# Wide weight units, earlier first loads and moved side work in a two-layer encoder step

## The chip, the cores and the metric

The kernel runs on one core of a Trainium2 chip. Five engines work in parallel, each with its own instruction queue that is taken strictly in order: TensorE (matrix products and transposes into PSUM), VectorE and ScalarE (element work), GpSimd (element work and some DMA issues), and SyncE (SP), which issues most DMAs. The metric is device time in microseconds, of the whole program. Three runs of the kernel before gave 2964.94, 2965.09 and 2965.37 us.

## The reference

Two groups of tokens, a prompt of 256 and a sample of 64, go through two layers with the same weights; here they are one block of 320 columns. All is in fp32.

```python
# layer 0: one projection, then A (8 query heads, 2 key heads, rotary, window 128, sinks)
#          and B (8 heads, own chunk + 8 before, relative bias), one output projection
h = x @ w_in_ab ; qa, ka = rope(...), rope(...)
out = concat(band_attention(A), band_attention(B)) @ w_out_ab
# layer 1: low-rank queries and keys with a rotary part, chunk-causal attention
# every layer:
x = layer_norm(ALPHA * x + mix, ln1_g, ln1_b)
x = layer_norm(ALPHA * x + square(relu(x @ w_up)) @ w_down, ln2_g, ln2_b)
gate = sigmoid(x @ w_ple_gate + b_ple_gate)
x = x + gate * (p @ w_ple)
```

The model width is 2048 (16 k-blocks of 128), the hidden width 8192. Outputs are the two results and the new caches.

## The kernel before, in words

**Layout.** Activations lie transposed: a tile has 128 features on the partitions and 320 tokens as columns. Each product is made of three matmuls: a value is split into a high part (a ScalarE copy to the rounded format fp32r) and a low part (a VectorE subtraction), and high x high, high x low and low x high are summed in PSUM. In names, `hl` is such an activation pair, `sf` and `t` are plain fp32 tiles, `mm` and `ax` are PSUM banks (five and three), `st` holds statistics.

**Weights.** `Weights` holds a list of units in the order of use. A unit has 128 rows times 1024 numbers: `wr` is what a DMA brought (four buffers), `ws` the split pair (four buffers). A unit is split in two slices of 512 numbers for each partition; `hi` is the ScalarE half and `lo` the VectorE half of one. `pump` emits such halves between the matmuls of the units before, `split_next` emits one, and `need` those that a matmul is about to use.

**Groups.** `group` computes 4 column blocks (128 features each) over all k-blocks, 12 matmuls for each k-block. `group8` does 8 column blocks at once, 24 matmuls for each k-block; it is used where the input appears tile by tile behind a norm: the first up projection and the first half of the gate, in both layers. Its units are planned by `plan_pair`: two units side by side, each of 2 k-blocks by 512 columns.

**Order.** The program is written out by a planner, `Sched`: it keeps an estimated clock for each engine (a VectorE operation of 320 columns counts 0.41 us), and side work is a generator that gives back when it wants to go on. `sch.tick()` after each few matmuls lets due generators emit their next instructions. Nothing of these times is in the program: only the order is, and an engine runs an instruction as soon as its inputs are there.

**Norms.** `ln_finish` sums the columns by matmuls with `ones` (`colsum`), copies the sums to `st`, takes the root, spreads mean and scale over the partitions by transposes (`tokbcast`), and emits products of the small matrix `w_ple` (`fill`) on TensorE between these steps.

**Rotation.** `rope` copies the bank to a tile (ScalarE), makes the swapped and multiplied halves by GpSimd (`u`), and multiplies and adds on VectorE. In layer 0 it runs for the two key heads (`akv_done`) and eight query heads (`aq_done`), in layer 1 for the rotary parts.

**Gate.** `gate_done` for tile `mt`: sigmoid (ScalarE), one product and two additions (VectorE), then a split for layer 1, or, in the last layer, transposes and output stores.

**Layer 1.** `residual` adds the two parts of each of the 16 inputs of layer 1 on GpSimd, for the output projection much later. It is added to the planner behind the group `cq`.

**Start.** `load_x` brings x in four pieces of 512 columns, three tiles each; `trans_x` transposes one k-block of it, `x_ready` keeps two k-blocks ahead of the first group, `akv`.

Of the kernel before, what the change touches and what calls it, by code (L numbers as in the profile page):

```python
# [33 lines left out]
KT = 16  # L34
# [142 lines left out]
class Weights:  # L177
# [23 lines left out]
    def plan_pair(self, key, w, c0):  # L201

        for r in range(0, D, 256):
            for h in range(2):
                a = w[r:r + 256, c0 + h * 512:c0 + (h + 1) * 512]
                self.unit(key, a.rearrange("(k p) c -> p k c", p=128), 2, 512)
# [9 lines left out]
    def dma(self):  # L216
# [6 lines left out]
        else:  # L223
            self.k.nc.sync.dma_start(out=t, in_=a)
# [3 lines left out]
    def hi(self):  # L228
        i, k0, k1 = self.slices[self.nhi]
        while self.ndma <= i:  # L230
            self.dma()
        if k0 == 0:
# [4 lines left out]
        self.k.S.activation(out=self.spl[i][:, 0, k0:k1], in_=self.raw[i][:, k0:k1], func=AF.Copy)  # L237
# [4 lines left out]
    def lo(self):  # L242
        i, k0, k1 = self.slices[self.nlo]
# [5 lines left out]
        self.k.V.tensor_tensor(out=s[:, 1, k0:k1], in0=r[:, k0:k1], in1=f32(s[:, 0, k0:k1]), op=ALU.subtract)  # L249
        self.nlo += 1  # L250
        sch.ready = keep
        if k1 == self.units[i][2]:
            del self.raw[i]
# [21 lines left out]
    def take(self, key):  # L275
        self.cur += 1
        assert self.units[self.cur][0] == key, (self.units[self.cur][0], key)
        self.spl.pop(self.cur - 1 - self.lag, None)
# [3 lines left out]
    def need(self, kk):  # L282

        while self.nlo < len(self.slices):
            i, k0, k1 = self.slices[self.nlo]
# [10 lines left out]
def trunk_kernel(ctx: ExitStack, tc: tile.TileContext, a, o):  # L296
# [116 lines left out]
    def plan_mlp(i):  # L413
        for c in range(8):
            if c == 0:
                ws.plan_pair(f"up{i}0", a["w_mlp_up"][i], 0)
# [10 lines left out]
        ws.plan_pair(f"gate{i}0", a["w_ple_gate"][i], 0)  # L427
# [82 lines left out]

    def load_x(ch):
        for j in range(3):
            t = slot_f((128, 512))
            n = 128 if j < 2 else 64
            if j == 2:
                G.memset(t[64:], 0.0)
            src = a["x_prompt"][0, j * 128:(j + 1) * 128] if j < 2 else a["x_sample"][0]
            nc.sync.dma_start(out=t[:n], in_=src[:, ch * 512:(ch + 1) * 512])
# [5 lines left out]
    ws.dma()  # L524
    ws.dma()
    ws.dma()
    load_x(1)
    ws.dma()

# [107 lines left out]
    def group8(key, rhs, done, need):  # L637

        ps = []
        ws.lag = 1  # L640
        for i in range(KT):
            need(i)
            kk = i % 2
            if kk == 0:
                ws.take(key)
                w0 = ws.spl[ws.cur]
                w1, _ = ws.take(key)
            ws.need(kk)
            ws.pump(2)
            x = rhs(i)  # L650
            w = lambda u, mm: (w0, w1)[mm // 4][:, u, kk, mm % 4 * 128:mm % 4 * 128 + 128]
# [1353 lines left out]
```

## Time and profile before

| | us |
|---|---|
| median of 3 runs | 2965.09 |
| the profiled execution | 2965.06 |
| its span | 2963.3 |
| TensorE busy in it | 2930.4 |
| VectorE / ScalarE / GpSimd busy | 1737.1 / 1299.4 / 221.6 |
| read from HBM, mean rate | 418.22 MB, 145 GB/s |

The span is the time from the first to the last recorded instruction. Busy times say which engine is the densest, not what each wait costs; for that the waits of TensorE are to be read, and the stretches in which its granted clock is 0.5 (1.2 GHz) instead of 1.0 (2.4 GHz). Before 14.45 us no clock is recorded, so the first stretch is read from the spacing of matmuls.

### The profile page before, as it was taken

To read this page: it belongs to the slowest core of one execution; us is meant where nothing else is said; L and a number is where in the kernel's file an instruction comes from. 1 tells how busy PE (TensorE), PEld (TensorE's weight loads), DVE (VectorE), ACT (ScalarE), POOL (GpSimd) and SP (SyncE) were. 2 spreads that over 40 slices of the span, in tenths; PEclk is the share of its full clock that TensorE was granted. 3 is DMA by queue.
4 is the path that set the end of the run, shared out by engine and by line. 5 is a ranking of instruction groups with operands and counts; after the bars stand their busy time and mean duration, and the time that the engine had idled before them with its cause. 6 is when DMAs were issued, how large, how long until landed. Compare 5 with 4: busy or idle time off the path is not lost.

```text
span 2963.3 us, 51140 instructions
## 1 busy us (share of the span) xinstructions
PE 2930.4 (99%) x20241; PEld 2922.5 (99%) x20241; DVE 1737.1 (59%) x3446; ACT 1299.4 (44%) x2745; POOL 221.6 (7%) x290
## 2 busy tenths in 40 slices
PE   9999999999999999999999999999999999999999
PEld 8999999999999999999999999999999999999998
DVE  5666677544444444557667676775444444444675
ACT  4455445344343343345455455453343343343453
POOL 2110020000000000011003110200000000000201
PEclk9999999999999999999999999999999999999999
DMA  7445444544444444444453323454444444444444
GB/s 237 135 152 166 150 142 137 164 149 146 155 150 148 153 150 151 150 137 145 144 149 112 102 79 105 130 158 154 149 147 151 155 146 145 161 149 144 143 146 118
DMA packets 284496, 430.17 MB, mean 145 GB/s; under 512 B 34518, under 2 KB 110024, under 8 KB 284256
## 3 DMA queue, kind: packets, MB, share of 16 engines
q1 hardware_dynamic: 280224, 416.75, 45.0%
q0 software_dynamic: 4032, 10.16, 1.0%
q8 instruction: 158, 2.59, 0.3%
q14 instruction: 82, 0.67, 0.1%
HBM read 418.22 MB, written 10.72 MB: 145 GB/s over the span
## 4 chain that ended last, share of the span: by engine, by line
PE 96%; DVE 2%; ACT 1%; DMA 1%; issue 0%; SPq 0%; ACTq 0%; POOL 0%; DVEq 0%; POOLq 0%
PE mm L386 27%; PE mm L388 27%; PE mm L387 27%; PE mm L664 1%; PE mm L663 1%; PE mm L665 1%; PE mm L620 1%; PE ax L402 1%; DVE t L172 1%; PE ax L664 1%; PE ax L663 1%; PE ax L665 1%; PE ax L388 1%; PE ax L387 1%; PE ax L386 0%
## 5 line engine op out<-in xcount | busy, mean ns | idle before, releaser
L386 PE MATMUL mm<-hl,ws 128*128 128x320 f32 x5608 | 1746.1, 311 | 1.9 <-DVE qz L172 1.3
L388 PE MATMUL mm<-hl,ws 128*128 128x320 f32 x5608 | 1733.4, 309 | 4.4 <-DVE ws L172 4.4
L387 PE MATMUL mm<-hl,ws 128*128 128x320 f32 x5608 | 1732.7, 309 | 0.0
L172 DVE TENSOR_TENSOR ws<-wr,ws 128x512 fp32r<-128x512 f32 (+1 forms) x1568 | 1045.1, 702 | 607.0 <-ACT ws L172 600.2
L172 ACT ACTIVATE ws<-wr 128x512 fp32r<-128x512 f32 (+1 forms) x1568 | 912.5, 620 | 1113.6 <-PE mm L388 860.8
L388 PEld LDWEIGHTS mm<-hl,ws 128*128 128x128 f32 x5608 | 1054.7, 188 | 5.2 <-DVE ws L172 5.2
L386 PEld LDWEIGHTS mm<-hl,ws 128*128 128x128 f32 x5608 | 1055.4, 188 | 4.1 <-DVE sf L172 1.8
L387 PEld LDWEIGHTS mm<-hl,ws 128*128 128x128 f32 x5608 | 1055.6, 188 | 0.0
L172 DVE TENSOR_TENSOR sf<-sf,mm 128x320 f32<-128x320 f32 x272 | 123.4, 487 | 204.6 <-PE mm L388 204.1
L172 POOL TENSOR_TENSOR t<-sf 128x320 f32<-128x320 f32 x8 | 7.5, 940 | 1871.6 <-DVE sf L172 1871.6
L172 DVE TENSOR_TENSOR t<-t 128x320 f32<-128x320 f32 x128 | 58.2, 489 | 123.3 <-ACT t L172 123.3
L665 PE MATMUL mm<-hl,ws 128*128 128x320 f32 x300 | 92.7, 309 | 0.0
L663 PE MATMUL mm<-hl,ws 128*128 128x320 f32 x300 | 92.7, 309 | 0.0
L664 PE MATMUL mm<-hl,ws 128*128 128x320 f32 x300 | 92.7, 309 | 0.0
L172 POOL TENSOR_TENSOR t<-t,sf 32x320 f32<-32x320 f32 (+2 forms) x72 | 77.4, 1074 | 197.5 <-ACT t L172 156.3
L172 ACT ACTIVATE t<-mm 128x320 f32<-128x320 f32 (+1 forms) x141 | 61.3, 435 | 50.2 <-PE mm L388 43.9
L172 DVE TENSOR_TENSOR sf<-sf,t 128x320 f32<-128x320 f32 x131 | 77.4, 612 | 2.9 <-ACT t L172 2.9
L172 ACT ACTIVATE hl<-ax 128x256 fp32r<-128x256 f32 (+3 forms) x110 | 33.0, 328 | 104.0 <-PE ax L402 42.7
L172 DVE TENSOR_TENSOR hl<-ax,hl 128x256 fp32r<-128x256 f32 (+3 forms) x110 | 36.4, 353 | 66.7 <-ACT hl L172 66.0
L172 DVE TENSOR_TENSOR hl<-t,hl 128x320 fp32r<-128x320 f32 (+1 forms) x152 | 68.8, 481 | 0.1
L172 ACT ACTIVATE hl<-t,PC 128x320 fp32r<-128x320 f32 x64 | 36.0, 563 | 72.4 <-DVE t L172 72.4
L172 ACT ACTIVATE hl<-t 128x320 fp32r<-128x320 f32 (+1 forms) x152 | 64.8, 461 | 6.1 <-DVE t L172 5.8
(162 smaller groups left out, 2042.7 us busy)
## 6 DMA issues: line engine op xcount, KB each, us to landing
wr<-in_w_mlp_up_dram SPq DMA_DIRECT2D x256, 512.0 KB, 3.7
wr<-in_w_mlp_down_dram SPq DMA_DIRECT2D x256, 512.0 KB, 4.1
wr<-in_w_ple_gate_dram SPq DMA_DIRECT2D x64, 512.0 KB, 3.7
wr<-in_w_in_ab_dram SPq DMA_DIRECT2D x114, 256.0 KB, 3.1
wr<-in_w_out_ab_dram SPq DMA_DIRECT2D x32, 512.0 KB, 3.9
wr<-in_w_out_c_dram SPq DMA_DIRECT2D x32, 512.0 KB, 3.8
wr<-in_w_kv_b_c_dram SPq DMA_DIRECT2D x16, 512.0 KB, 3.7
wr<-in_w_in_ab_dram SPq DMA_DIRECT2D x15, 512.0 KB, 5.1
```

The costliest lines, as they stand in the source:

```text
L172: return f(*args, **kw)
L386: P.matmul(out, wh, xh, start=start, stop=False)
L387: P.matmul(out, wh, xl, start=False, stop=False)
L388: P.matmul(out, wl, xh, start=False, stop=stop)
L402: P.transpose(out, in_, ident if n == 128 else ident[:n, :n])
L620: P.matmul(ps[mm][:, :T], w[:, u, kk, mm * 128:(mm + 1) * 128], x[:, v], start=z, stop=False)
L663: P.matmul(o_, w(0, mm), x[:, 0], start=False, stop=False)
L664: P.matmul(o_, w(1, mm), x[:, 0], start=False, stop=False)
L665: P.matmul(o_, w(0, mm), x[:, 1], start=False, stop=i == KT - 1)
```

## The change

- `plan_wide` takes the place of `plan_pair`: a unit is one k-block by 1024 columns, and its slices are the two column halves. `group8` takes one unit for each k-block. In `ln_finish` one more `split_next` stands ahead of the copy of the sums.
- `gate_done` gives back for 2000 ns times the tile's number ahead of its VectorE work, for the first eight tiles; the wait ahead of the last layer's transposes is gone.
- `rope_p` takes the place of `rope` in layer 0: the two halves are swapped by two ScalarE copies out of PSUM, and all products are VectorE's.
- `residual` is added behind `ckv`, ahead of `ckr` and `cq`, with a delay of 1000 in place of 3000.
- The first pieces of x have 256 columns; two weight units are issued from ScalarE's queue; 20 transposes of the identity stand first on TensorE; only one k-block of x is transposed ahead of the first split; the memsets of x tiles go to VectorE.

```diff
+    def plan_wide(self, key, w, c0):
+        for r in range(0, D, 128):
+            self.unit(key, w[r:r + 128, c0:c0 + 1024].rearrange("(k p) c -> p k c", p=128), 1, 1024)
...
-        step = max(1, SLICE // ncols)
+        step, wide = max(1, SLICE // ncols), min(SLICE, ncols)
         for k0 in range(0, nk, step):
-            self.slices.append((i, k0, min(nk, k0 + step)))
+            for c0 in range(0, ncols, wide):
+                self.slices.append((i, k0, min(nk, k0 + step), c0, c0 + wide))
...
+    XC = (0, 256, 512, 1024, 1536, 2048)
     load_x(0)
-    ws.dma()
-    ws.dma()
-    ws.dma()
+    ws.dma(nc.scalar)
+    ws.dma(nc.scalar)
     load_x(1)
     ws.dma()
+    load_x(2)
+    ws.dma()
+    warm = aux()
+    for _ in range(20):
+        P.transpose(warm[:, 0:128], ident, ident)
+    free()
...
     def group8(key, rhs, done, need):
         for i in range(KT):
             need(i)
-            kk = i % 2
-            if kk == 0:
-                ws.take(key)
-                w0 = ws.spl[ws.cur]
-                w1, _ = ws.take(key)
-            ws.need(kk)
+            w, _ = ws.take(key)
+            ws.need(0)
             ws.pump(2)
...
+    def rope_p(src, tab, dst, u):
+        copy(u[0:64], src[64:128, :T])
+        copy(u[64:128], src[0:64, :T])
+        V.tensor_tensor(out=dst, in0=src[:, :T], in1=tab[:, 0], op=ALU.mult)
+        yield
+        V.tensor_tensor(out=u, in0=u, in1=tab[:, 1], op=ALU.mult)
+        V.tensor_tensor(out=dst, in0=dst, in1=u, op=ALU.subtract)
...
-    x_ready(0)
+    trans_x(0)
+    ws.hi()
+    x, ax = xq[0]
+    V.tensor_tensor(out=x[:, 1], in0=ax[:, :T], in1=f32(x[:, 0]), op=ALU.subtract)
+    xT[0] = x
+    ws.lo()
     group("akv", 4, lambda i: xT[i], akv_done, need=x_ready)
...
-            copy(t, ps[:, :T])
-            yield
-            yield from rope(t, ropeA, r, 64)
+            yield from rope_p(ps, ropeA, r, t)
...
         colsum(ax, 3, L.sq, 0)
         ws.split_next()
+        ws.split_next()
         V.tensor_copy(st[:, 0:6], ax[:107, 0:6])
...
                 if ax:
                     free()
-                yield
+                yield 2000 * mt if mt < 8 else None
...
-                if mt < 8:
-                    yield 500 + 1000 * mt
...
     group("ckv", 4, lambda i: x3[i], ckv_done)
-    group("ckr", 4, lambda i: x3[i], ckr_done)
-    group("cq", 3, lambda i: x3[i], lambda m, ps: cq_done(3 + m, ps))
...
-    sch.add(residual(), 3000)
+    sch.add(residual(), 1000)
+    group("ckr", 4, lambda i: x3[i], ckr_done)
+    group("cq", 3, lambda i: x3[i], lambda m, ps: cq_done(3 + m, ps))
```

**The first score of layer 0.** TensorE's order in the group `b0`, which follows the rotated queries. Before: `hl_191` is x's fourth k-block, `ax_997` the first score, `hl_955` a key or query pair of head 0.

```order
L386 MATMUL mm_923<-hl_191,ws_843 128x320
L387 MATMUL mm_923<-hl_191,ws_843 128x320
L388 MATMUL mm_923<-hl_191,ws_843 128x320
L386 MATMUL ax_997<-hl_661,hl_955 128x128
L387 MATMUL ax_997<-hl_661,hl_955 128x128
L388 MATMUL ax_997<-hl_661,hl_955 128x128
L386 MATMUL ax_997<-hl_661,hl_955 128x256
L387 MATMUL ax_997<-hl_661,hl_955 128x256
L388 MATMUL ax_997<-hl_661,hl_955 128x256
```

After: `hl_278` is x's sixth k-block, `ax_1069` the same score.

```order
L386 MATMUL mm_955<-hl_278,ws_901 128x320
L387 MATMUL mm_955<-hl_278,ws_901 128x320
L388 MATMUL mm_955<-hl_278,ws_901 128x320
L386 MATMUL ax_1069<-hl_669,hl_994 128x128
L387 MATMUL ax_1069<-hl_669,hl_994 128x128
L388 MATMUL ax_1069<-hl_669,hl_994 128x128
L386 MATMUL ax_1069<-hl_669,hl_994 128x256
L387 MATMUL ax_1069<-hl_669,hl_994 128x256
L388 MATMUL ax_1069<-hl_669,hl_994 128x256
```

The score stood behind 42 matmuls of this group (three k-blocks and half of the fourth), and stands behind 72 (six k-blocks).

**The norm ahead of layer 0's gate.** ScalarE's order. Before: `ws_14242` is the gate's first unit (k-blocks 0 and 1, columns 0 to 511), `ws_14374` its second (columns 512 to 1023), `ws_14378` its third; `hl_14324`, `hl_14329` and `hl_14371` are the first three tiles of the normed input.

```order
L172 ACTIVATE hl_14329<-t_14326,PC 128x320
L172 ACTIVATE sf_14339<-mm_14332 128x320
L172 ACTIVATE sf_14339<-mm_14341 128x320
L172 ACTIVATE ws_14242<-wr_14134 128x512
L172 ACTIVATE sf_14358<-mm_14351 128x320
L172 ACTIVATE sf_14358<-mm_14360 128x320
L172 ACTIVATE hl_14371<-t_14368,PC 128x320
L172 ACTIVATE ws_14374<-wr_14171 128x512 x2
L172 ACTIVATE ws_14378<-wr_14208 128x512 x2
L172 ACTIVATE hl_14422<-t_14419,PC 128x320
```

After: `ws_14253`, the first k-block, is converted in both halves some rows above these; `ws_14304` is the second k-block; `st_14295` is the root in the norm.

```order
L172 ACTIVATE sf_14285<-mm_14287 128x320
L172 ACTIVATE ws_14304<-wr_14182 128x512
L172 ACTIVATE st_14295<-st_14295 107x3
L172 ACTIVATE sf_14322<-mm_14315 128x320
L172 ACTIVATE t_14328<-ax_14324 128x320
L172 ACTIVATE sf_14322<-mm_14332 128x320
L172 ACTIVATE hl_14347<-t_14345,PC 128x320
L172 ACTIVATE t_14344<-ax_14340 128x320
L172 ACTIVATE hl_14352<-t_14349,PC 128x320
L172 ACTIVATE sf_14362<-mm_14355 128x320
L172 ACTIVATE sf_14362<-mm_14364 128x320
L172 ACTIVATE ws_14304<-wr_14182 128x512
```

Before, both ScalarE halves of the second unit (`ws_14374`) came behind the third tile. After, the two halves of the second k-block stand ahead of it, one of them ahead of the root; VectorE's halves stand likewise.

**Layer 0's gate.** VectorE's order behind the first half of the gate. Before: `t` are the gate's tiles, `sf` their products with `w_ple`, and `ws_15002` the first weight unit split behind the gate's work.

```order
L172 TENSOR_TENSOR t_14979<-t_14979,hl_14501 128x320 x2
L172 TENSOR_TENSOR t_14987<-t_14987,sf_5395 128x320
L172 TENSOR_TENSOR t_14987<-t_14987,hl_14536 128x320 x2
L172 TENSOR_TENSOR hl_14989<-t_14945,hl_14989 128x320
L172 TENSOR_TENSOR t_14997<-t_14997,sf_5395 128x320
L172 TENSOR_TENSOR t_14997<-t_14997,hl_14575 128x320 x2
L172 TENSOR_TENSOR ws_15002<-wr_14854,ws_15002 128x512
L172 TENSOR_TENSOR hl_15016<-t_14950,hl_15016 128x320
L172 TENSOR_TENSOR hl_15035<-t_14955,hl_15035 128x320
L172 TENSOR_TENSOR ws_15002<-wr_14854,ws_15002 128x512
```

After: `ws_14960` and `ws_15015` are the third and fourth unit of the gate's next group.

```order
L172 TENSOR_TENSOR ws_14960<-wr_14840,ws_14960 128x512
L172 TENSOR_TENSOR t_14967<-t_14967,sf_5320 128x320
L172 TENSOR_TENSOR t_14967<-t_14967,hl_14347 128x320 x2
L172 TENSOR_TENSOR ws_14960<-wr_14840,ws_14960 128x512
L172 TENSOR_TENSOR t_14975<-t_14975,sf_5320 128x320
L172 TENSOR_TENSOR t_14975<-t_14975,hl_14352 128x320 x2
L172 TENSOR_TENSOR hl_15005<-t_14967,hl_15005 128x320
L172 TENSOR_TENSOR ws_15015<-wr_14877,ws_15015 128x512
L172 TENSOR_TENSOR t_14980<-t_14980,sf_5356 128x320
L172 TENSOR_TENSOR t_14980<-t_14980,hl_14394 128x320 x2
L172 TENSOR_TENSOR hl_15030<-t_14975,hl_15030 128x320
L172 TENSOR_TENSOR ws_15015<-wr_14877,ws_15015 128x512
```

Before, the operations of all eight tiles stood ahead of the first weight half; after, a weight half stands behind nearly each tile.

## Rows read from the trace of the kernel before

**Rows 1.** The page: TensorE's busy time; three groups: busy, mean ns | idle.
```profile
PE 2930.4 (99%) x20241; PEld 2922.5 (99%) x20241; DVE 1737.1 (59%) x3446; ACT 1299.4 (44%) x2745; POOL 221.6 (7%) x290
...
L172 DVE TENSOR_TENSOR ws<-wr,ws 128x512 fp32r<-128x512 f32 (+1 forms) x1568 | 1045.1, 702 | 607.0 <-ACT ws L172 600.2
...
L172 DVE TENSOR_TENSOR t<-t 128x320 f32<-128x320 f32 x128 | 58.2, 489 | 123.3 <-ACT t L172 123.3
...
L172 ACT ACTIVATE t<-mm 128x320 f32<-128x320 f32 (+1 forms) x141 | 61.3, 435 | 50.2 <-PE mm L388 43.9
```

**Rows 2.** Waits of TensorE: us in total, times, longest us.
```profile
PE mm L656 <- ACT ws L172: 8.4, 4, 2.1
PE mm L388 <- DVE ws L172: 4.4, 2, 3.0
PE mm L402 <- DMA sf<-in_x_prompt_dram: 3.7, 1, 3.7
PE ax L388 <- DVE hl L172: 3.0, 1, 3.0
...
PE mm L402 <- DMA sf<-in_x_sample_dram: 1.5, 1, 1.5
PE ax L402 <- DVE hl L172: 1.3, 1, 1.3
PE mm L386 <- DVE qz L172: 1.3, 2, 0.7
...
PE ax L402 <- DVE st L172: 0.9, 1, 0.9
PE ax L693 <- DVE t L172: 0.9, 1, 0.9
```

**Rows 3.** Stretches: length, busy of PE, PEld, DVE, ACT, POOL, granted clock, DMA share.
```profile
82.70:89.60 6.90, 6.31 (x24) 6.31 (x25) 6.58 (x24) 3.72 (x13) 1.80 (x4) 0.51 0.61 193
1369.50:1373.00 3.50, 3.50 (x16) 3.50 (x15) 3.38 (x8) 2.12 (x5) 0.00 (x0) 0.51 0.46 154
```

**Rows 4.** The chain that ended last: start us, us, what.
```profile
1.67 4.36 DMA sf<-in_x_sample_dram
...
6.61 0.64 PE ax L402 x3
...
8.94 3.57 PE mm L620 x12
...
319.72 1.76 PE mm L620 x12
```

**Rows 5.** Timeline at the start: start us, us, engine, instruction.
```profile
1.02 0.29 POOL masks.py:199 TENSOR_SCALAR_AFFINE_SELECT ident<-ident 128x128 f32<-128x128 f32 x1
...
14.28 0.40 PE L388 MATMUL mm<-hl,ws 128*128 128x320 f32 x1
```

**Rows 6.** Timeline behind the group `aq0`, GpSimd and VectorE.
```profile
73.20 9.15 POOL L172 TENSOR_TENSOR t<-sf,sf 64x320 f32<-64x320 f32 x8 [12.73 <-ACT sf L172]
...
78.12 1.16 DVE L172 TENSOR_TENSOR sf<-sf,t 128x320 f32<-128x320 f32 x1
...
82.82 1.02 DVE L172 TENSOR_TENSOR hl<-sf,hl 128x256 fp32r<-128x256 f32 x4
```

**Rows 7.** Timeline at the norm ahead of layer 0's gate, ScalarE and VectorE.
```profile
1368.31 2.18 ACT L172 ACTIVATE ws<-wr 128x512 fp32r<-128x512 f32 x4
...
1360.32 0.17 DVE L172 COPY st<-ax 107x6 f32<-107x6 f32 x1 [0.68 <-PE ax L693]
...
1371.28 0.55 DVE L172 SCALAR_TENSOR_TENSOR t<-sf,PC,t 128x320 f32<-128x320 f32 x1
```

**Rows 8.** Timeline of VectorE behind layer 0's gate.
```profile
1424.55 1.02 DVE L172 TENSOR_TENSOR t<-t,hl 128x320 f32<-128x320 f32 x2
...
1436.07 0.68 DVE L172 TENSOR_TENSOR ws<-wr,ws 128x512 fp32r<-128x512 f32 x1
```

**Rows 9.** Timeline of GpSimd behind the group `cq`.
```profile
1561.08 16.57 POOL L172 TENSOR_TENSOR sf<-hl 128x320 f32<-128x320 f32 x16
```

More of the change, by code (lines that the diff above doesn't have):

```diff
@@ L199, in plan @@
             self.unit(key, a.rearrange("(k p) c -> p k c", p=128), nk, ncols)
[L201 to L206, printed above, removed]
+    def plan_wide(self, key, w, c0):
+        for r in range(0, D, 128):
+            self.unit(key, w[r:r + 128, c0:c0 + 1024].rearrange("(k p) c -> p k c", p=128), 1, 1024)
     def unit(self, key, a, nk, ncols):
@@ L228, in hi @@
     def hi(self):
-        i, k0, k1 = self.slices[self.nhi]
+        i, k0, k1, c0, c1 = self.slices[self.nhi]
         while self.ndma <= i:
             self.dma()
-        if k0 == 0:
+        if k0 == 0 and c0 == 0:
             key, a, nk, nc_ = self.units[i]
@@ L242, in lo @@
     def lo(self):
-        i, k0, k1 = self.slices[self.nlo]
+        i, k0, k1, c0, c1 = self.slices[self.nlo]
         while self.nhi <= self.nlo:
@@ L248, in lo @@
         keep, sch.ready = sch.ready, self.hi_end[self.nlo]
-        self.k.V.tensor_tensor(out=s[:, 1, k0:k1], in0=r[:, k0:k1], in1=f32(s[:, 0, k0:k1]), op=ALU.subtract)
+        self.k.V.tensor_tensor(out=s[:, 1, k0:k1, c0:c1], in0=r[:, k0:k1, c0:c1],
+                                in1=f32(s[:, 0, k0:k1, c0:c1]), op=ALU.subtract)
         self.nlo += 1
         sch.ready = keep
-        if k1 == self.units[i][2]:
+        if k1 == self.units[i][2] and c1 == self.units[i][3]:
             del self.raw[i]
@@ L284, in need @@
         while self.nlo < len(self.slices):
-            i, k0, k1 = self.slices[self.nlo]
+            i, k0 = self.slices[self.nlo][:2]
             if i > self.cur or (i == self.cur and k0 > kk):
@@ L426, in plan_mlp @@
         plan_ple(i, 3)
-        ws.plan_pair(f"gate{i}0", a["w_ple_gate"][i], 0)
+        ws.plan_wide(f"gate{i}0", a["w_ple_gate"][i], 0)
         for g in range(2, 4):
@@ L655, in group8 @@
                     for mm in range(8):
-                        P.matmul(ps[mm][:, :T], w(u, mm), x[:, v], start=u + v == 0, stop=False)
+                        P.matmul(ps[mm][:, :T], w[:, u, 0, mm * 128:(mm + 1) * 128], x[:, v], start=u + v == 0, stop=False)
                         sch.now += 147
@@ L661, in group8 @@
             for mm in range(8):
-                o_ = ps[mm][:, :T]
-                P.matmul(o_, w(0, mm), x[:, 0], start=False, stop=False)
-                P.matmul(o_, w(1, mm), x[:, 0], start=False, stop=False)
-                P.matmul(o_, w(0, mm), x[:, 1], start=False, stop=i == KT - 1)
+                o_, c = ps[mm][:, :T], slice(mm * 128, (mm + 1) * 128)
+                P.matmul(o_, w[:, 0, 0, c], x[:, 0], start=False, stop=False)
+                P.matmul(o_, w[:, 1, 0, c], x[:, 0], start=False, stop=False)
+                P.matmul(o_, w[:, 0, 0, c], x[:, 1], start=False, stop=i == KT - 1)
                 sch.now += 441
@@ L959, in trans_x @@
     def trans_x(kt):
-        ch, c = divmod(kt, 4)
+        ch = next(i for i in range(5) if kt * 128 < XC[i + 1])
+        c = kt - XC[ch] // 128
         ax = aux() if kt % 2 else bank()
@@ L971, in x_ready @@
         if i in (2, 5):
-            load_x(2 if i == 2 else 3)
+            load_x(3 if i == 2 else 4)
         if i == 6:
             nc.sync.dma_start(out=ropeA, in_=a["ropeA"])
-        while len(xq) < min(i + 3, KT):
+        while len(xq) < min(i + 3 if i else 2, KT):
             trans_x(len(xq))
@@ L1037, in akv_done @@
         if m < 2:
-            t = tmp()
-            copy(t, ps[:, :T])
-            yield
-            yield from rope(t, ropeA, kfA[:, m], 64)
+            yield from rope_p(ps, ropeA, kfA[:, m], tmp())
             yield
@@ L1067, in f @@
             t, r = tr[:, 0], tr[:, 1]
-            copy(t, ps[:, :T])
-            yield
-            yield from rope(t, ropeA, r, 64)
+            yield from rope_p(ps, ropeA, r, t)
             yield
@@ L1755, in trunk_kernel @@
     group("ckv", 4, lambda i: x3[i], ckv_done)
-    group("ckr", 4, lambda i: x3[i], ckr_done)
-    group("cq", 3, lambda i: x3[i], lambda m, ps: cq_done(3 + m, ps))
-    sch.until(lambda: all(c is not None for c in Cs.ckv) and Cs.past)
     LC = ln_new()
@@ L1770, in trunk_kernel @@
     Cs.res = False
-    sch.add(residual(), 3000)
+    sch.add(residual(), 1000)
+    group("ckr", 4, lambda i: x3[i], ckr_done)
+    group("cq", 3, lambda i: x3[i], lambda m, ps: cq_done(3 + m, ps))
+    sch.until(lambda: all(c is not None for c in Cs.ckv) and Cs.past)
     SCC = 192 ** -0.5
```

22 lines of the change are left out of this document (9 added, 13 removed).

## The prediction

> **What bounds the kernel now.** I read the page first: TensorE is busy for 2930.4 of 2963.3 us [rows 1]. So nothing that VectorE, ScalarE or GpSimd save counts by itself. Only three things can move the end: the waits of TensorE, the stretches in which it runs at the lower of its two clock levels, and the ends of the program. The reader is to see in [rows 1] that the rest is one dense stream of matmuls, and the change takes none of them away.
>
> Second I read TensorE's list of waits [rows 2]. It has a few places only: 8.4 us in four waits of 2.1 us each on a ScalarE weight half, 4.4 us in two on a VectorE weight half, 3.7 and 1.5 us at the start, 3.0 us in layer 0 before a score matmul, and small ones of about 1 us.
>
> Third come the stretches of the clock [rows 3]. After the wait at 80 us the granted clock is 0.5 (1.2 GHz) for 6.9 us, and after the wait at 1367 for 3.5 us. The stretches 1437.8 to 1441.2 and 2837.3 to 2840.7, behind two more of the waits, read like the second one. At 1.2 GHz half of such a stretch is lost: 3.4 us for the first, 1.7 us for each of the other three. A wait of 2 to 3 us can therefore cost 4 to 6. The start is slow too: twelve matmuls take 3.57 us there and 1.76 us later [rows 4], and the matmuls come at the fast spacing only from 14.3 us [rows 5].
>
> The sum is made against the profiled execution: 2963.3 us of span and 1.8 around it, 2965.06; the median of the runs, 2965.09, is the same number.
>
> **The start.** Before, the first matmul that does work stands at 8.94 us [rows 4]: it is behind the third load of x (issued at 1.67, landed 4.36 later), three transposes for each of three k-blocks, three ScalarE copies and a conversion of 0.55 (four took 2.18, [rows 7]). Now the first pieces of x are half as wide, two weight units are issued from ScalarE's queue beside them, and a single k-block's x copy stands ahead of its weight half. Against that, twenty transposes of the identity stand first on TensorE. The identity is there at 1.31 us [rows 5]; a transpose at the low level takes 0.64 / 3 = 0.21 us [rows 4], so they end near 1.35 + 20 x 0.213 = 5.6 us. Six real ones follow (1.3 us, to 6.9), the x copy after the first three (0.435, [rows 1]) and the weight half (0.55) give a first matmul at about 7.5, 1.4 us earlier.
> The rest is the clock. Before, 5.4 us of matmuls from 8.94 to 14.3 at half speed did 2.7 us of full-speed work. If the level rises when the first matmul comes, the new start is ahead by 3.7 us in all; if it needs the same 5.4 us of matmuls again, by about 1. I take 2.0, and keep 0.3 and 3.7. The four memsets on VectorE lie in its idle start.
> The Trainium skill ("TensorE: Matmul & The Clock Gate", Part 4: PE-mode transpose) says that transposes do not count towards the clock gate as matmuls do. No run here shows it yet; by that rule the twenty transposes warm nothing, and the term would be some 1 us instead of 2.
>
> **Layer 0 rotation.** Before, four heads' rotation is eight GpSimd instructions, 9.15 us from 73.20 [rows 6]. VectorE's work beside them is slowed: an addition takes 1.16 us where it takes 0.489 elsewhere [rows 1, 6]. So the low halves of the queries come at 82.82, and TensorE waits 3.0 us [rows 2]. Now each head is two ScalarE copies (0.435 each, however few partitions) and three VectorE operations. Four heads: 8 x 0.435 = 3.5 us on ScalarE; on VectorE 12 x 0.489 = 5.9, four weight halves at 0.70 = 2.8 between them, and the low half itself. From 72.7 on (GpSimd's start less one copy) it is there near 81.9. TensorE came to the first score at 80, 3 us before that half. In its order the score has moved from the 43rd matmul of the next group to the 73rd, 30 x 0.147 (1.76 / 12, [rows 4]) = 4.4 us later, to 84.4. Both are in time: 3.0 us and the 3.4 us of low clock go, 6.4.
> What is late next is a PSUM bank. It is held for two copies instead of one: the third of four heads is freed 6 x 0.435 = 2.6 us after its group's first result, and the next group wants it some 2.4 after, behind a conversion at worst. I book 0.2 us for each of the four groups that rotate (bounds 0 and 0.5): 0.8. The term is 5.6. The rest of layer 0 is interleaved anew, since the order comes from estimates of these durations; its two small entries of 1.3 us [rows 2] I leave as they are.
>
> **The blocks behind the norms.** Four times (two up projections, two gates) the first k-block's eight columns came from two units, and ScalarE converted the second unit only behind an x tile: four conversions from 1368.31 [rows 7], when TensorE had already stood for some 1.5 us. Now one unit holds the whole first k-block, and by ScalarE's order both its halves and half of the next unit are converted before the norm's square root. The 8.4 us go, and with them the two low stretches behind them (1369.5 and 2837.3), 3.4.
> The new slice costs something: its subtraction stands on VectorE before the copy of the sums (the row at 1360.32). There VectorE waited 0.68 us, but ScalarE must first finish two gate inputs and then convert (0.55), so the copy and with it the transposes of mean and scale come 0.7 us later. TensorE has fill matmuls between them; 0.4 us is left each time (bounds 0 and 0.8), 1.6 in all. Beyond the first block nothing starves: a k-block is 24 matmuls, 3.52 us, and VectorE needs two slices and three norm steps for it, 2 x 0.70 + 3 x 0.55 = 3.05 at most [rows 1, 7]. The term is 8.4 + 3.4 - 1.6 = 10.2.
>
> **The gate's eight tiles.** Before, VectorE runs three operations for each of eight tiles without a break; the first pair stands at 1424.55, the first weight half at 1436.07 [rows 8]. TensorE used up what was prepared and waited 3.0 us (1.5 in layer 1, together the 4.4 of [rows 2]). Now the tiles start 2 us apart in the planner's time, and VectorE's order has a weight half after nearly each tile. Eight tiles with their splits are 32 x 0.489 = 15.7 us, the ten weight halves among them 7.0: 22.7 us, in which TensorE uses one half each 1.76 us, 13. Five halves stood ahead, which with the ten makes 15: 3.5 us of lead at its end, and by the same count not under 2 on the way. In layer 1 the tiles' transposes stand on TensorE some 0.3 to 0.5 us behind the end of their tile's additions; I book nothing for them (bounds 0 and 1). 4.4 and 1.7 of low clock go: 6.1.
>
> **Residual sums.** Sixteen GpSimd additions, 16.57 us from 1561.08 [rows 9], slowed VectorE just where the sums of squares and the first key/value block needed it: 0.9 and 0.9 us of TensorE [rows 2]. They now stand two groups earlier in GpSimd's queue, ahead of three output DMAs, for which nothing waits soon, and of the rotary key's rotation, which the first scores of layer 1 need a group later. Their inputs are ready tile by tile, so several run at once, beside the gate work. Six of them at 1.04 us cost VectorE about 0.67 each (1.16 less 0.489), 4 us against a lead of 2 to 3.5 there. I take 1.8 gained, and keep as the other end a new wait of 1.6 us with 1.7 of clock.
> The Trainium skill ("SBUF — State Buffer", Who interferes with whom) says that a VectorE instruction with two SBUF inputs contends with a GpSimd instruction that reads SBUF, and that one with a PSUM input does not. The 1.16 against 0.489 us agrees. By it the moved sums do slow the gate's additions, and the first step of the new rotation is free of them.
>
> **Sum.** 2.0 + 5.6 + 10.2 + 6.1 + 1.8 = 25.7; 2965.1 - 25.7 = 2939.4 us.
>
> **Rivals.**
> 1. The reordered layer 0 waits elsewhere. TensorE takes its instructions in order, so a score or transpose that the planner sets too early stops it, as at 80 us: 3.0 and 3.4 us. For it: VectorE's operations are longer than the planner assumes (0.49 us against 0.41), and 30 matmuls of slack came by chance. Against it: without GpSimd beside it VectorE is nearer to the plan. One or two places: 2946 to 2952.
> 2. The transposes warm nothing and the first weights come no sooner, since all loads share one set of queues: the start gains 0.3 instead of 2.0. 2941.
> 3. The moved sums and the gate work meet, and the wait of 3.0 us with its low clock is back in layer 0 in part: 1.6 + 1.7 lost. 2943.
> 4. Slower than before: the wide units halve VectorE's slack. It prepares one k-block at a time; if a block cost it more than 3.52 us, TensorE would wait at every one of 4 x 15 blocks. It loses to before from 3.52 + 25.7 / 60 = 3.95 us, a third over the 3.05 above, for instance with GpSimd beside it throughout; at 4.1 us the time is 2939 + 35 = 2974. Against it: it is the same work for each k-block as before, where no wait followed the first block, and GpSimd has nothing to do there.
>
> **How the numbers follow.** Forecast 0.61, its own range 2935 to 2944; rival 1 0.20; rival 2 0.10; rival 3 0.06; rival 4 0.03. The lower end of the range takes the start at 3.7, no cost for banks and slices, and the small entries of layer 0 gone: 25.7 + 1.7 + 2.4 + 2.6 = 32.4, 2932.7. The upper end holds rival 1 with two places, 2951. The bound of same is 0.2%, 5.9 us, about what a measurement of this kernel can tell from no change. Slower: rival 4 less its milder part, 0.02; same: 0.03; faster 0.95.
>
> **What would show it.** Right: no entry on ScalarE's weight halves in the waits of the first matmuls of a wide block; no granted clock under 1.0 at 82, 1369, 1437 and 2837 us (shifted); weight halves between the gate's additions on VectorE; GpSimd with no rotation before 1500 us; first work at 7.5 us. Wrong: a wait of 2 us or more anywhere in 40 to 450 us, or a start whose twelve matmuls still take 3.5 us and stand at 9 us. The forecast falls if the list of waits of TensorE still sums to over 15 us.

## The result, and the profile after

The changed kernel takes 2944.32 us (median of 4 runs, 2943.49 to 2945.16) against 2965.23 (2964.94 to 2966.45): ratio 0.9929, interval 0.9911 to 0.9946, 20.9 us less. Forecast were 25.7 less. The profiled execution is the one of 2945.16, span 2943.4, 19.9 us shorter than that of before. Two of the kernels below each had one far slower execution (8809 and 8811 us), which their medians leave out.

TensorE's waits of the changed kernel, which answer to [rows 2] (us in total, times, longest):

```profile
PE ax L402 <- ACT t L172: 2.1, 1, 2.1
PE ax L402 <- DVE t L172: 1.8, 1, 1.8
PE ax L537 <- POOL ident masks.py:199: 1.4, 1, 1.4
PE mm L386 <- DVE qz L172: 1.2, 2, 0.7
PE mm L630 <- ACT hl L172: 0.9, 2, 0.4
PE mm L630 <- ACT ws L172: 0.7, 1, 0.7
PE ax L813 <- DVE hl L172: 0.7, 1, 0.7
PE mm L386 <- DVE sf L172: 0.6, 3, 0.2
PE ax L387 <- DVE pt L172: 0.6, 1, 0.6
PE mm L386 <- ACT ws L172: 0.3, 1, 0.3
PE mm L402 <- DMA sf<-in_x_sample_dram: 0.2, 1, 0.2
```

The four waits on a ScalarE weight half (8.4), the two on a VectorE half (4.4), the one before the first score (3.0) and the two at the residual sums (1.8) are gone. The first line is new, and so are the small ones on ident, `hl`, `sf` and `pt` tiles (4.2 us together). The whole list sums to 10.5 us; the forecast was to fall at over 15. Stretches of the changed kernel (length, busy time of PE, PEld, DVE, ACT, POOL, granted clock, DMA share, GB/s), to be held against [rows 3]:

```profile
75.00:90.00 15.00, 15.00 (x108) 14.99 (x107) 13.37 (x42) 7.85 (x25) 0.44 (x4) 1.00 0.51 158
1350.00:1375.00 25.00, 24.85 (x175) 24.33 (x174) 20.24 (x43) 14.45 (x32) 0.00 (x0) 1.00 0.45 153
1420.00:1445.00 25.00, 25.00 (x172) 25.00 (x171) 24.52 (x42) 12.43 (x25) 6.74 (x6) 1.00 0.37 125
2873.90:2877.30 3.40, 3.40 (x16) 3.36 (x15) 2.52 (x7) 1.32 (x3) 0.00 (x0) 0.50 0.46 154
```

The old low stretches are gone and one is new, behind the new wait. Its place is the last layer's gate. TensorE there, and then ScalarE ahead of it (start us, us, instruction, in brackets the idle time before it and what ended it):

```profile
2873.51 0.56 PE L402 MATMUL ax<-ident,t 128*128 128x128 f32 x3 [2.14 <-ACT t L172]
```

```profile
2868.37 1.15 ACT L172 ACTIVATE ws<-wr 128x512 fp32r<-128x512 f32 x2 [2.37 <-issue]
2869.54 1.28 ACT L172 ACT_TABLE_LOAD   x1
2870.84 2.20 ACT L172 ACTIVATE t<-mm,PC 128x320 f32<-128x320 f32 x5
2872.90 0.97 ACT L172 ACTIVATE t<-ax,PC 128x320 f32<-128x320 f32 x2
```

The first transposes of the gate's tiles stand ahead of the three matmuls of its eighth column. They need a bank of the `ax` kind, and the wide gate holds all eight banks. The first `ax` bank is read by the sixth sigmoid, which ends near 2873.4; 0.1 us later the transposes start. The sigmoids begin late, because ScalarE stood 2.37 us before two conversions and then loaded a table. The profile names nothing that the conversions waited for; they start 0.1 us after the last matmul of the k-block before ends (2868.28), so a `ws` buffer that TensorE still read is the likely reason.

The start, TensorE (it answers to [rows 4, 5]):

```profile
1.37 4.53 PE L537 MATMUL ax<-ident 128*128 128x128 f32 x20 [1.37 <-POOL ident masks.py:199]
6.86 0.49 PE L402 MATMUL ax<-ident,sf 128*128 128x128 f32 x3
8.07 2.17 PE L630 MATMUL mm<-hl,ws 128*128 128x320 f32 x12 [0.72 <-ACT ws L172]
```

Three transposes of x take 0.49 us at 6.86, where three took 0.64 in [rows 4]: the clock had risen while nothing but transposes had run.

Gained time by place, worked out from the two traces as the change in the lead of the same weight matmul (its start before less its start after):

| term | forecast | measured |
|---|---|---|
| start, to 30 us | 2.0 | 2.9 |
| layer 0, to 438 | 5.6 | 3.7 |
| wide blocks | 10.2 | 1.84 + 3.37 + 1.84 + 3.36 - 2 x 0.96 = 8.5 |
| gates | 6.1 | 4.76 - 2.21 = 2.55 |
| residual sums | 1.8 | 2.1 |
| sum | 25.7 | 19.7 |

The other 0.2 us of the span come behind the last weight matmul. The two 0.96 are lost where the first down projection begins, behind each wide up block (the two waits of 0.4 us on an `hl` tile are part of it).

### The profile page after: what moved, and what is told of

Its sections match the earlier page's. It is cut to its first block, busy times and chain, and to the rows that moved or that the text cites. A ratio compares the mean times of both kernels' runs of the same rounds, so it can differ in the third digit from the quotient of the medians.

```text
span 2943.4 us, 51190 instructions
## 1 busy us (share of the span) xinstructions
PE 2927.8 (99%) x20261; PEld 2917.2 (99%) x20261; DVE 1746.3 (59%) x3461; ACT 1298.9 (44%) x2755; POOL 198.0 (7%) x266
## 4 chain that ended last, share of the span: by engine, by line
PE 97%; ACT 1%; DVE 1%; issue 1%; DMA 0%; SPq 0%; ACTq 0%; DVEq 0%; POOLq 0%; POOL 0%
PE mm L386 28%; PE mm L388 28%; PE mm L387 28%; PE mm L667 1%; PE mm L666 1%; PE mm L668 1%; PE ax L402 1%; PE mm L630 1%; PE ax L667 1%; PE ax L668 1%; PE ax L666 1%; PE ax L387 1%; PE ax L388 1%; PE ax L386 0%; PE ax L841 0%
## 5 line engine op out<-in xcount | busy, mean ns | idle before, releaser
L172 POOL TENSOR_TENSOR t<-t,sf 32x320 f32<-32x320 f32 (+1 forms) x68 | 73.4, 1080 | 203.1 <-ACT t L172 178.3
L172 ACT ACTIVATE t<-mm 128x320 f32<-128x320 f32 (+2 forms) x143 | 61.2, 434 | 30.2 <-PE mm L388 29.3
```

The costliest lines, as they stand in the source:

```text
L172: return f(*args, **kw)
```

## The experiments

Each was timed beside the kernel before. Medians, of four to ten executions, are compared with the 2944.3 above; what an edit gains or loses at a place is its lead over the changed kernel's profile, worked out like the table. The changed kernel's own four runs fall into two pairs, 2943.5 and 2943.6, 2945.0 and 2945.2. Only the last has a trace, with the low stretch at 2873.9; that the faster pair lacks this stretch is likely but not shown. In the run with the residual sums back and in that with GpSimd's rotation and later scores, the same wait of 2.14 us stands at the same matmul and no stretch follows. A difference of 1.6 us can be that alone, so the places are read from the traces.

**The last gate's wait, moved.**

```diff
+                if mt < 8:
+                    yield 500 + 1000 * mt
                 yield from nat_k(s, w, ystg[mt - w], False)
```

> The changed kernel with the wait of 500 + 1000 ns times the tile's number put back ahead of the transposes of the last layer's first eight gate tiles. Theory (the transposes stand directly behind the last block of the wide gate, where the tile's sums come 2.1 us too late, and the wait costs 1.7 us more at the low clock): no wait and no granted clock of 0.5 near 2871 us, 3.8 us gained, 2940.5 us against 2944.3. Rival (the wait only moves: the transposes later meet the rest of the gate's tiles and the weight halves on VectorE, as in the kernel before, where TensorE waited 1.5 us there): 2942.5 or more, with a wait on a VectorE weight half behind the wide gate.

Measured 2945.0: nothing gained. TensorE now has six more matmuls ahead of the transposes, as in the kernel before, waits 1.27 us, without a low stretch, and starts them at the same moment:

```profile
2873.52 0.55 PE L402 MATMUL ax<-ident,t 128*128 128x128 f32 x3 [1.27 <-ACT t L172]
```

So not the tile's sums set it (they end 0.5 us earlier, at 2872.95) but the bank. The gain was given back 30 us later: the later transposes moved four GpSimd sums and the last tiles' additions on VectorE together, and TensorE waits twice there, 1.9 us together. VectorE then, with GpSimd busy from 2902.99 for 4.19 us beside it:

```profile
2903.35 0.97 DVE L172 TENSOR_TENSOR t<-t,sf 128x320 f32<-128x320 f32 x1 [1.02 <-ACT t L172]
2904.36 2.12 DVE L172 TENSOR_TENSOR t<-t,hl 128x320 f32<-128x320 f32 x2
...
2908.50 0.48 DVE L172 TENSOR_TENSOR t<-t,sf 128x320 f32<-128x320 f32 x1
```

The same operation takes 0.97 us beside GpSimd and 0.48 without it. The theory fell, the rival held in kind.

**The table loaded early.**

```diff
+            if i == 12 and key.startswith("gate"):
+                S.preload_act_table(AF.Sigmoid)
```

> The changed kernel with the sigmoid's table loaded ahead of the thirteenth k-block of each wide gate, so that its 1.28 us lie in ScalarE's idle time. Theory (the chain that the first transposes of the last gate wait for begins on ScalarE, where a conversion that waits for a weight buffer and the table load stand ahead of the first sigmoid and make it 2.6 us late): the wait of 2.1 us there becomes 0.8 to 1.1, the low clock behind it may go too: 2941.5 to 2943.3. Rival (the transposes simply stand too early, or wait for VectorE, whatever ScalarE does before): the wait stays at 2 us, 2944.3.

Measured 2942.45. The sigmoids begin 1.25 us earlier, the transposes start right behind the first `ax` sigmoid again, the wait is 0.72 and no low stretch follows; 3.0 us are gained at this place, of which 1.4 are the shorter wait and the rest the stretch. First ScalarE, then TensorE:

```profile
2868.53 1.15 ACT L172 ACTIVATE ws<-wr 128x512 fp32r<-128x512 f32 x2 [2.37 <-issue]
2869.59 2.18 ACT L172 ACTIVATE t<-mm,PC 128x320 f32<-128x320 f32 x5
2871.64 0.97 ACT L172 ACTIVATE t<-ax,PC 128x320 f32<-128x320 f32 x2
```

```profile
2872.24 0.55 PE L402 MATMUL ax<-ident,t 128*128 128x128 f32 x3 [0.72 <-ACT t L172]
```

**No warm transposes.** The twenty transposes are taken out.

> The changed kernel without the twenty transposes of the identity at the start. Theory (they are why the granted clock is 1.0 from 6.72 us on, ahead of the first matmul that does work): without them the first twelve matmuls take 3.5 us instead of 2.2 and the clock rises some 5 us later, 2.0 to 2.7 us lost, 2946.3 to 2947.0. Rival (transposes do not count for the clock, the rise at 6.72 has another cause, and the start gained from the loads alone): 2944.3 and the same 2.2 us for the first twelve matmuls.

Measured 2948.14, but only 1.1 us of it at the start: the first work stands at 8.36 us in place of 8.07, the first twelve matmuls take 2.92 us in place of 2.17, and the first record of the full clock is at 10.35 us (6.72 with the transposes):

```profile
7.10 0.85 PE L402 MATMUL ax<-ident,sf 128*128 128x128 f32 x3
8.36 2.92 PE L626 MATMUL mm<-hl,ws 128*128 128x320 f32 x12 [0.41 <-ACT ws L172]
```

The rest, 1.8 us, is a low stretch at 232.2, behind gaps of 0.9 and 0.6 us that the changed kernel has too (0.7 and 0.6), there without one. The transposes are worth half of what was expected; that they raise the clock stands.

**The rotation back on GpSimd.** `rope` in place of `rope_p`.

> The changed kernel with the rotation of layer 0 on GpSimd again, as in the kernel before; the first score then stands again behind 42 matmuls of its group. Theory (that part removed a wait of 3.0 us and 3.4 us of low clock and added three bank waits of some 0.45 us): the wait of about 3 us and the clock of 0.5 come back near 77 us, the three short waits near 43 and 73 us go, 4.6 us lost: 2948.9. Rival (the wait hung on the early loads or on other side work that is gone now): under 1 us lost or a gain of 1.4, 2943 to 2945.

Measured 2946.92. The wait of 3.0 us is back, with a low stretch of 3.4 us at 81.3 (3.9 lost there); the short bank waits are gone (0.55 gained from 30 to 70 us, 0.9 just after). The theory's signs hold, the net is smaller.

**One slice less ahead of the sums.**

```diff
         colsum(ax, 3, L.sq, 0)
-        ws.split_next()
         ws.split_next()
```

> The changed kernel with one weight slice split, in place of two, ahead of the copy of the column sums in each norm. Theory (the second slice holds that copy up and costs TensorE some 0.4 us at each of the four norms; the blocks behind the norms have their weights in time without it): about 1.6 us gained, 2942.7 us against 2944.3, with the losses of 0.7 us near 446, 1355, 1863 and 2812 us down to 0.3. Rival (that slice is what brings the first k-block's last ScalarE half in time): TensorE waits for a ScalarE weight half at the wide blocks again, by 0.5 us or more each, 2946 or more.

Measured 2942.45. Its profile is of the execution of 8809 us, so no trace of this kernel can be held against the others at the norms; the same edit within the combination below gains 0.32 to 0.34 at each of the four. No wait on a ScalarE weight half comes back there: the rival falls.

**The residual sums back.** `residual` again behind `cq`, with 3000.

> The changed kernel with the sixteen GpSimd residual sums behind the group cq again, as in the kernel before. Theory (beside them VectorE's work with two SBUF inputs takes twice as long just where the sums of squares are wanted): TensorE's waits of 0.9 us on an st tile and 0.9 us on a t tile come back near 1555 us, 1.9 us lost, 2946.2. Rival (those waits had gone with something else, or the sums cost as much in their new place): 2944.3 within 0.7.

Measured 2945.99, all five within 0.15 us. The waits are back at their old place, 2.4 us lost there:

```profile
PE ax L704 <- DVE t L172: 1.2, 1, 1.2
PE ax L402 <- DVE st L172: 0.9, 1, 0.9
```

**One copy out of the bank.**

```diff
-        copy(u[0:64], src[64:128, :T])
-        copy(u[64:128], src[0:64, :T])
-        V.tensor_tensor(out=dst, in0=src[:, :T], in1=tab[:, 0], op=ALU.mult)
+        copy(dst, src[:, :T])
+        copy(u[0:64], dst[64:128])
+        copy(u[64:128], dst[0:64])
+        V.tensor_tensor(out=dst, in0=dst, in1=tab[:, 0], op=ALU.mult)
```

> The changed kernel in which layer 0's rotation copies the whole bank to SBUF once on ScalarE and swaps the halves and multiplies from that copy. Theory (each bank is held for two ScalarE copies and then a VectorE product, 1.35 us, and TensorE's three waits of 0.2 us near 43 and 73 us, with 0.45 us each in the spacing of the matmuls, are for these banks): the three waits go, 1.0 to 1.4 us gained, 2943.0. Rival (the third ScalarE copy for each head makes the low halves of the queries late): a wait before the first score near 83 us, of 1 us or more, 2945.5 or more.

Measured 2945.35, and both theories missed: the bank waits grew, to 3.2 us in four. (1.2 us of its profile are lost at the start, where no edit was made; see the last section.) The next head's copy out of its bank stands behind the swaps of the head before, on ScalarE:

```profile
72.42 0.44 ACT L172 ACTIVATE sf<-mm 128x320 f32<-128x320 f32 x1 [1.52 <-PE mm L388]
72.89 0.95 ACT L172 ACTIVATE sf<-sf 64x320 f32<-64x320 f32 x2
73.87 0.44 ACT L172 ACTIVATE sf<-mm 128x320 f32<-128x320 f32 x1
```

**GpSimd's rotation with later scores.** `rope` again, and

```diff
+                if h == 1:
+                    yield 4400
                 launch(Ah[h - 1:h + 1])
```

> The changed kernel with layer 0's rotation on GpSimd again, but the first pair of scores given to the planner 4.4 us later, so that it stands behind some 70 matmuls of its group, as in the changed kernel. Theory A (the wait of 3.0 us came of where the score stood, and GpSimd's rotation is hidden if the score stands later): no wait at the score, and no bank waits either, 1 us gained against the changed kernel, 2943.3. Theory B (the rotation on GpSimd, and VectorE slowed beside it, is what was late, and what follows the queries waits for it elsewhere): a wait of 1 us or more within 20 us of the score, 2945.5 or more.

Measured 2943.31 (2941.98 to 2944.22); in the trace it is 2.2 us ahead of the changed kernel by 360 us. GpSimd takes as long as in [rows 6], and the first score waits 0.44 and 0.45 us. GpSimd, then TensorE:

```profile
70.29 9.20 POOL L172 TENSOR_TENSOR t<-sf,sf 64x320 f32<-64x320 f32 x8 [12.71 <-ACT sf L172]
```

```profile
82.49 0.33 PE L386 MATMUL ax<-hl,hl 128*128 128x128 f32 x1 [0.44 <-ACT hl L172]
...
83.38 0.33 PE L388 MATMUL ax<-hl,hl 128*128 128x128 f32 x1 [0.45 <-DVE hl L172]
```

Theory A holds: the later place is enough without the new rotation. Nor does the new rotation bring the low halves sooner. VectorE's first four of them, in the changed kernel and then here:

```profile
80.45 1.02 DVE L172 TENSOR_TENSOR hl<-sf,hl 128x256 fp32r<-128x256 f32 x4
```

```profile
79.97 1.02 DVE L172 TENSOR_TENSOR hl<-sf,hl 128x256 fp32r<-128x256 f32 x4
```

**The same edit alone, in the kernel before.**

> The kernel before with one edit: its first pair of scores is given to the planner 4.4 us later, so that the score stands behind 75 matmuls of its group in place of 42; the rotation stays on GpSimd. Theory (what the change won in layer 0 came of the score's place, not of the faster rotation): the wait of 3.0 us on a VectorE low half near 80 us and the low clock behind it go, 5 to 6 us gained, 2959.5 us against some 2965. Rival (without the other edits the rotation's end is late for the next instruction too): a wait of 1 us or more within 20 us of the score and less than 3.5 us gained, 2961.5 or more.

Measured 2960.80 against 2964.36. Between 70 and 360 us it gains 5.65 us, as expected (it had lost 0.23 at the start). Then 1.54 are lost: behind a wait of 2.09 us at 450.38, which the kernel before has with the same length at 455.78, the clock falls here and did not there:

```profile
450.50:453.90 3.40, 3.40 (x13) 3.40 (x14) 3.36 (x7) 2.00 (x5) 0.00 (x0) 0.50 0.52 152
```

**Six edits together.** GpSimd's rotation, later scores, the early table, one slice less, and the two below; the delays of `gate_done` in the last layer follow the new order of columns.

```diff
-            for mm in range(8):
+            for mm in ((4, 5, 6, 7, 0, 1, 2, 3) if key == "gate10" and i == KT - 1 else range(8)):
...
-    trans_x(0)
-    ws.hi()
+    ws.hi()
+    trans_x(0)
```

> The changed kernel with six small edits: layer 0's rotation on GpSimd again with the first scores 4.4 us later, the sigmoid's table loaded ahead of the thirteenth k-block of the wide gates, the last layer's wide gate finishing its columns 4 to 7 first (so that the three banks of the kind that the transposes take come free first), one slice less ahead of the copy of the column sums, and the first weight half converted ahead of x's first copy. Theory (each removes the wait it was made for, 1.5 + 1.4 + 0.5 + 1.3 + 0.45 us, and none of them meets another): 2938.5 us, the wait at the last gate's first transposes under 0.4 us. Rival (the bank was not what those transposes waited for: the sums on VectorE are): that wait stays at 0.7 us or more, 2939.5; if the later scores, or fewer slices ahead, meet another wait, 2941 or more.

Measured 2938.69 (2938.47 to 2939.09), ratio to before 0.9911, interval 0.9898 to 0.9925. By place: 0.4 at the start, 2.0 in layer 0, 1.3 at the norms, 3.4 at the last gate; 0.4 are given back behind the last weight matmul. With the `ax` columns first a bank is free before the first sums end on VectorE, at 2867.82. The transposes start 0.15 us after that, with a wait of 0.30, so these sums probably set them now, although the profile names a sigmoid, the last one to end before (2867.92). VectorE, ScalarE, TensorE:

```profile
2866.80 1.02 DVE L172 TENSOR_TENSOR t<-t,hl 128x320 f32<-128x320 f32 x2
```

```profile
2866.14 1.35 ACT L172 ACTIVATE t<-ax,PC 128x320 f32<-128x320 f32 x3
```

```profile
2867.97 0.52 PE L402 MATMUL ax<-ident,t 128*128 128x128 f32 x3 [0.30 <-ACT t L172]
```

**The conversions behind the fourth column.** The combination, and in a wide block's last k-block `pump(2)` goes from its head to `pump(3)` behind its fourth column.

> The kernel of the run before this one, and in the last k-block of each wide block the conversions for later units stand on ScalarE and VectorE behind its fourth column, not ahead of its first. Theory (a conversion that waits for a buffer that TensorE still reads holds up the relus, and so the first input of the down projection, 0.9 us lost at each of two places, and the sigmoids too): TensorE's waits of 0.4 us on hl tiles near 503 and 1959 us go, 1.2 to 1.8 us gained against that run. Rival (the weights for the next group then come late): a wait on a ws tile behind the wide blocks, no gain or up to 2 us lost.

Measured 2942.59, 3.9 lost. At the down projections the loss grows by 1.6 us each. The conversions now stand among the relus, and the squares (the four below) behind them. VectorE:

```profile
500.34 1.29 DVE L172 TENSOR_TENSOR ws<-wr,ws 128x512 fp32r<-128x512 f32 x2 [1.35 <-ACT ws L172]
501.55 1.69 DVE L172 TENSOR_TENSOR t<-t 128x320 f32<-128x320 f32 x4
```

Neither theory had this place right.

**The old units behind the norms.** `plan_pair` and the old `group8` in the changed kernel; its second `split_next` stays.

> The changed kernel with the units of two k-blocks by 512 columns again behind the norms; the second slice ahead of the copy of the column sums stays. Theory (one unit for the whole first k-block is what removed the four waits of 2.1 us and the low clock behind two of them, and it put the conversions that hold up ScalarE at the end of each wide block): the four waits on a ScalarE weight half come back at 1.3 to 2.1 us each with 1.7 to 3.4 us of low clock, the two losses of 0.9 us ahead of the down projections go, and the last gate's wait of 2.1 us is shorter: 5 to 8 us lost, 2949 to 2952. Rival (the second slice ahead of the copy would have been enough): the waits come back at under 1 us each, under 3 us lost, 2947 or less.

Measured 2939.88 (2939.58 to 2941.25): 4.4 us faster than the changed kernel. The theory falls; of the rival the reason holds (the second slice is enough), not the loss. No wait on a ScalarE weight half comes back behind the norms, and the leads at the four norms are the changed kernel's within 0.01 us. ScalarE at the first norm, in the kernel before and then here:

```profile
447.72 0.20 ACT L172 ACTIVATE st<-st 107x3 f32<-107x3 f32 x1 [1.20 <-DVE st L172]
...
455.12 2.18 ACT L172 ACTIVATE ws<-wr 128x512 fp32r<-128x512 f32 x4
```

```profile
439.86 0.62 ACT L172 ACTIVATE ws<-wr 128x512 fp32r<-128x512 f32 x1
441.71 0.21 ACT L172 ACTIVATE st<-st 107x3 f32<-107x3 f32 x1 [1.23 <-DVE st L172]
...
448.82 1.66 ACT L172 ACTIVATE ws<-wr 128x512 fp32r<-128x512 f32 x3
```

One conversion stands ahead of the root (`st`) and no longer among those behind the third tile. At all four norms this is the only difference in ScalarE's order around the root.

The two 0.96 at the down projections are gained: the last conversions end there before the first relu, which starts at 500.34 us; in the changed kernel two conversions start at 499.94, behind a wait for the k-block before, and the relus at 501.00. At the last gate 3.5 are gained, some 1.7 of them the low stretch: there ScalarE converts and loads the table early and stands ready for the first column.

```profile
2862.97 1.15 ACT L172 ACTIVATE ws<-wr 128x512 fp32r<-128x512 f32 x2 [0.61 <-ACT ws L172]
2864.14 1.28 ACT L172 ACT_TABLE_LOAD   x1
2866.88 2.29 ACT L172 ACTIVATE t<-mm,PC 128x320 f32<-128x320 f32 x5 [1.46 <-PE mm L682]
```

The wide unit was not needed: with the old units, one more slice ahead of the copy of the sums is enough. With wide units that slice is not needed either, by the time of the run with one slice less and the trace of the combination. Old units with a single slice, beside the other edits, were not run; that the waits would then come back is read from ScalarE's order alone. The old units within the six-edit combination were not tried either.

## Why the prediction was right, and where it was wrong

The direction and most of the size came from the right view: the list of TensorE's waits and the low stretches behind them, place by place. By its own steps:

**Start: right, a little small.** Booked 2.0, measured 2.9. The bounds 3.7 and "about 1" do not follow from their own terms: 1.4 us earlier with 2.7 or 0 of clock is 4.1 or 1.4. The first work stands at 8.07, not at 7.5 (x's transposes end at 7.35 and not at 6.9, and the weight half queues behind x's copy), but the clock was up by then, nearer to the upper bound. The rival that transposes warm nothing fell: without them 1.1 us is lost there and the full clock is first recorded 3.6 us later. The other 1.8 us of the 2.9 came with the loads and the single k-block, which no run took apart.

**Layer 0: the gain was there, its reason was wrong and its cost too small.** Booked were 6.4 less 0.8, measured 3.7. The text let the 3.0 and 3.4 us go because the low half would come earlier and the score stood later, "both are in time". The runs part the two: with GpSimd's rotation and the later score the wait all but goes (0.9 us left), and in the kernel before this single line brought 5.65 us. The later place did it. It came with the change by the planner's estimates and not by design; the text took it as a second reason, and that was luck. The low halves are there at 80.45 us, against 79.97 with GpSimd's rotation, so the first reason gave nothing. The new rotation only costs, because its banks are held for two copies and then a VectorE product that starts behind them. That the rotation was slow on GpSimd was true and did not matter. The 0.8 booked for bank holds was too little: 0.6 us near 43 and 0.9 near 73 are lost beyond the normal spacing, and some more at the later query groups; by 360 us the run with GpSimd's rotation and later scores is 2.2 us ahead.

**Blocks behind the norms: the gain was right, its cause only one of two.** 10.4 us came there, against 11.8 less 1.6. "Now one unit holds the whole first k-block", from which "The 8.4 us go" was drawn, holds for wide units with a single slice; but the last experiment has the old units and none of the waits. The slice that I had booked as a cost only (1.6; it costs 1.3 beside wide units) is a remedy too, because it puts one conversion ahead of the norm's root in ScalarE's order. With both, one of them is only a cost. The step that failed is "Beyond the first block nothing starves": the wide units cost 2 x 0.96 at the down projections, where I booked nothing, and the wait at the last gate. It counted VectorE's work for a k-block and not ScalarE's conversions in front of the last block's first columns.

**Gates: layer 0 right, layer 1 wrong.** 4.76 measured for 4.7. No run took the new delays out, so that they removed the wait is argued; the wide units and the second slice did not, since the wait stays away without either. In layer 1, 1.5 were to be gained and 2.2 were lost, some 1.7 of it the low stretch: this is the largest miss, 3.7 us. The step was "In layer 1 the tiles' transposes stand on TensorE some 0.3 to 0.5 us behind the end of their tile's additions; I book nothing for them". That was read from the planner's times, which know no table load (1.28 us) and no conversion that stands before a buffer in use, and it looked for the sums where the bank came last. In the kernel before six more matmuls stood ahead of the transposes, and ScalarE had loaded the table before the first column came.

**Residual sums: right.** 1.8 booked, 2.1 measured, 2.4 when undone. They run at 1419 to 1485 now, one or two at a time, and TensorE is busy for all of 1420 to 1445, so the third rival did not come. In [rows 9] they stood in one row of sixteen.

Of the rivals, the first (the reordered program waits elsewhere, 2946 to 2952) was the nearest in kind, though the new wait came in the last gate and not in layer 0. The slower case did not come: no wait in a wide block behind its first.

## What to carry to other kernels

When a dense engine waits, first move the waiting instruction later in its order: one line did what a rewritten rotation was credited with. When an edit comes in two parts, undo each one alone before believing which of them worked. An order from a planner is only as good as the stalls that the planner knows; look in the trace for what it leaves out, such as table loads and a queue stopped before a buffer in use.

## What the hardware showed unexpectedly

The granted clock does not fall behind every wait of the same length. A wait of 2.09 us at the same matmul was followed by 3.4 us at 0.5 in one kernel (at 450.5) and by none in the other; small gaps near 230 us had such a stretch in one run and not in others. The wait of 2.14 or 2.15 us at the last gate stands in six profiles (the changed kernel's, no warm transposes, the rotation back, the residual sums back, one copy, later scores); a stretch of 3.4 us at 0.5 follows in four of them and none in two (the residual sums back, later scores). A stretch cost 1.5 to 1.9 us where the leads show it, and the four runs of the changed kernel differ by 1.4 to 1.7 in two pairs. Single times are therefore good to about one such step; 1.27 and 0.72 us of wait at the last gate were followed by none.

Transposes did raise the clock: with twenty transposes of the identity and two of x ahead, the full level is first recorded at 6.72 us, before any other matmul. In the run with one copy it is recorded at 4.64 us, when only the identity's had run. The Trainium skill ("TensorE: Matmul & The Clock Gate", Part 4: PE-mode transpose) says that they do not count as matmuls do; here, with fp32 transposes, the measurement differs, and it decides.

The raised level can be lost again just as the work begins. In that run, whose start has no edit, the clock fell to 0.5 at 8.05 us, behind waits of 0.95 and 0.72 us, for 3.4 us. The first twelve matmuls took 3.44 us there, and 1.2 us of the start's 2.9 were gone:

```profile
7.89 3.44 PE L630 MATMUL mm<-hl,ws 128*128 128x320 f32 x12 [0.72 <-ACT ws L172]
```

VectorE's additions with two SBUF inputs took 0.97 us beside GpSimd's sums and 0.48 behind them, in one stretch of 6 us. This agrees with the Trainium skill ("SBUF — State Buffer", Who interferes with whom).
